# A streaming encoder step on one core: the mix stored in two parts, memory's products begun earlier, one score bank for two heads, four early output products

## The chip, the cores and the metric

The kernel runs on one core of one Trainium2 chip. The metric is the device time of one launch in microseconds; the time before is the median of three runs, 1799.81 us (1794.37 to 1802.57). One further execution was recorded by the hardware profiler, and every duration of an instruction comes from it.

## The reference

One layer of a hybrid encoder for two request groups that share the weights: a prompt of 1024 frames and a sample of 64 frames with caches, both of width 1024. All inputs and outputs are float32.

```python
h = rms_norm(x, g_norm1)
qa, ka, va, qb, kb, vb, logf = in_proj(h, w_in, ...)     # 8 + 8 heads of 64, QK-norm, forget logits
xp = xp + concat(band_attn(qa, ka, va, rel_bias), forget_attn(qb, kb, vb, logf)) @ w_o
mk, mv = mem_kv(mem_prompt, g_mem, w_mkv, g_mk)          # 256 memory tokens, 4 heads of 256
xp = xp + mem_attend(rms_norm(xp, g_norm2), mk, mv, w_mq, g_mq, w_mo)
xp = xp + conv_ffn(rms_norm(xp, g_norm3), prev, w_up, w_conv, b_conv, w_down)
# the sample rows: the same, but attention over cache + new rows (512 for heads A, 1024 for heads B),
# memory from its own cache, convolution from its own state
```

Outputs are both y, and the new keys, values, forget logits, memory keys and values and convolution states.

## The kernel before, in words

A float32 product is made of three TensorE products of "fp32r" parts: every operand is split into a high part (`act.copy` into an fp32r tile) and a low part (operand minus high part, by VectorE or GpSimd), and hi·hi, lo·hi and hi·lo are summed in one PSUM bank. Prompt and sample stand side by side as N = 1024 + 64 columns.

The program is one straight list of instructions. Its stages:

1. **Projection and prompt attention** (to about 565 us). Head pairs are projected one after the other, eight token tiles each (`proj`); the attention of finished pairs (`Attn`, 256 queries at a time) is woven between its matmuls by `weave`, which spreads a list of small steps (`subs`) over a list of main steps. `Attn.sum` ends each pair's block: the two heads' outputs are put into a 128x256 tile `mix`, which is stored to the DRAM tensor `mixd`.
2. **End of attention, memory's keys and values.** Memory (256 tokens) times `w_mkv` is a `line` of 64 pieces of six matmuls (8 column blocks n, 2 token tiles t, 4 pieces c). `load_wm` and `split_wm` fetch and split the weights, `mem_end` normalises a finished block and stores it, `mem_turn` transposes a key block for the DRAM copy `kmd`. `LEFT` says how many pieces stand beside each of the last substeps of attention.
3. **Sample attention**: eight `Sample` objects (head pairs, in the order `SAMPLES`). In step x of the loop the scores of sample x are made, the softmax, transposes and sums of sample x-1 are finished, and the caches of sample x+1 are loaded and split; `PER[x]` pieces of memory's line are woven between. `score(h)` runs once per head. It writes into rows of both heads, of which only the head's own 64 rows are read.
4. **Output projection** `project`: 24 `Product`s (8 blocks m of 128 rows, 3 chunks of 384, 384 and 320 columns, in `ORDER`), each 24 matmuls. The operand is the mix, in two parts `mixr`, with the samples' columns last (chunk 2). A finished product is added to the residual, stored to `x1d`, split into h2 and squared for the next norm. `Stream` fetches and splits the weights ahead.
5. Memory cross attention, feed-forward network and output, up to the end. The change leaves these as they are.

In between, `open_left` (once the line is used up) takes the place of memory's tiles, and loads the mix back in eight loads of 512 KB, four of them in flight, which ScalarE and VectorE split into `mixr`. The first product belongs to the last pass of the sample loop, the second follows it. `mixd`, `x1d`, `kmd` and `vmd` are DRAM tensors.

What sets the order: each engine runs its own list in program order and waits where an operand is not ready or a tile is not free. All data transfers here are issued by SyncE (SP) in one ordered list; an issue that waits holds back those behind it. A tile pool opened in the place of a closed one waits for what the closed one's tiles did. PSUM has eight banks of 2 KB per partition: two `pj`, two `PT`, one `tq`, one `O`, two `S`.

The lines that the text speaks of (numbers of the kernel before): L272 projection matmuls, L453/L508 prompt scores and sums, L520 the mix's store, L591 to L605 memory's inputs and weight splits, L615 memory's matmuls, L634 to L649 their ends, L709/L710 cache splits, L730 sample score matmuls, L733/L735 their reductions, L757 to L784 sample transposes, sums and outputs, L852 w_o's low part, L869 output matmuls, L908 to L912 the mix's loads and splits, L998 to L1015 the residual and what follows a product.

## Time and profile before

| | |
|---|---|
| median of three runs | 1799.81 us (1794.37 to 1802.57) |
| profiled execution, own time | 1798.58 us |
| its span, first to last instruction | 1796.5 us |
| mean granted TensorE clock | 0.991 |
| TensorE matmuls busy | 1718.8 us (96%) |
| VectorE busy | 1225.0 us (68%) |
| ScalarE busy | 930.5 us (52%) |
| GpSimd busy | 662.8 us (37%) |
| DMA | 200.12 MB, mean 111 GB/s |
| TensorE busy from 600 to 700 us | 88.81 of 100 |
| TensorE busy from 700 to 750 us | 43.17 of 50 |

How to read it: PE is TensorE's matmuls, PEld its weight loads, DVE VectorE, ACT ScalarE, POOL GpSimd, SP SyncE. Times are microseconds from the first instruction. "idle <-X" names what ended an engine's idle time. A group of instructions has its line, engine, operation, written tile <- read tiles and shapes, then its total and mean time (ns). The granted clock is the share of full speed that TensorE was given.

### The profile page before, as it was taken

The numbers are of one execution on the slowest core, as the hardware profiler recorded it, in microseconds if no ns is written. First come the engines' busy times: TensorE is split into PE (matmuls) and PEld (weight loads), VectorE is DVE, ScalarE is ACT, GpSimd is POOL, SyncE is SP. The second block draws the span as 40 slices with busy tenths as digits, with TensorE's granted clock in tenths as the row PEclk, the third lists the DMA queues.
The fourth block names the chain that finished last, engine by engine and source line by source line (L and its number), as shares of the span: only waits on it lengthen the run. The fifth ranks groups of instructions, "written<-read, shape, count | busy, mean of one in ns | idle before, by whom it ended". The sixth has DMA issues, their size and how long they took to land.

```text
span 1796.5 us, 34030 instructions
## 1 busy us (share of the span) xinstructions
PE 1718.8 (96%) x12412; PEld 1663.7 (93%) x12412; DVE 1225.0 (68%) x2710; ACT 930.5 (52%) x2042; POOL 662.8 (37%) x1025
## 2 busy tenths in 40 slices
PE   6899999999997888999999999999999999999999
PEld 5789999999997777999999999999999999999999
DVE  5877667677676797433444379877777777677994
ACT  5646666677676567433554456343333333433332
POOL 5746657878776554453443612100000000000000
PEclk9999999999999999999999999999999999999999
DMA  8312122122113777541111563222222222794232
GB/s 285 96 46 72 36 76 79 50 72 74 48 54 97 222 229 213 163 141 60 54 54 59 150 219 103 73 79 78 85 86 84 73 73 72 268 304 151 77 118 80
DMA packets 134103, 200.12 MB, mean 111 GB/s; under 512 B 20824, under 2 KB 73944, under 8 KB 133936
## 3 DMA queue, kind: packets, MB, share of 16 engines
q1 hardware_dynamic: 133936, 197.96, 34.9%
q8 instruction: 97, 1.59, 0.4%
q14 instruction: 70, 0.57, 0.1%
HBM read 155.61 MB, written 45.44 MB: 112 GB/s over the span
## 4 chain that ended last, share of the span: by engine, by line
PE 46%; DVE 3%; DMA 2%; issue 2%; POOL 1%; ACT 1%; SPq 0%; POOLq 0%; ACTq 0%; DVEq 0%
PE W L1381 25%; PE W L1678 9%; PE pj L869 7%; PE W L869 2%; DMA raw<-in_w_down_dram 1%; PE S L1124 1%; PE tq L1160 1%; PE O L1160 1%; POOL lo L852 1%; DVE lo L1246 0%; PE PT L1147 0%; DVE f L1246 0%; PE O L1124 0%; DMA kvraw<-in_w_down_dram 0%; DMA h<-ad 0%
## 5 line engine op out<-in xcount | busy, mean ns | idle before, releaser
L272 PE MATMUL pj<-whi,xhi 128*128 128x384 f32 (+1 forms) x512 | 194.9, 381 | 8.2 <-ACT xhi L130 7.1
L272 PE MATMUL pj<-wlo,xhi 128*128 128x384 f32 (+1 forms) x512 | 176.9, 346 | 3.2 <-POOL wlo L123 2.9
L272 PE MATMUL pj<-whi,xlo 128*128 128x384 f32 (+1 forms) x512 | 175.1, 342 | 4.2 <-DVE xlo L131 4.2
L1487 POOL COPY s<-gp 128x2 f32<-128x2 f32 x22 | 15.8, 718 | 335.0 <-DVE gp L1486 335.0
L458 ACT ACTIVATE s<-s,mx 128x640 f32<-128x640 f32 (+7 forms) x128 | 94.2, 736 | 80.1 <-DVE mx L456 78.4
L1381 PE MATMUL W<-h,hi 128*128 128x272 f32 x704 | 134.4, 288 | 1.4 <-ACT qlo L1517 1.4
L1678 PE MATMUL W<-f,hi 128*128 128x272 f32 x672 | 128.3, 288 | 3.2 <-DVE f L1246 3.1
L495 DVE TENSOR_TENSOR ptl<-PT,pth 128x512 fp32r<-128x512 f32 (+2 forms) x192 | 99.6, 522 | 37.8 <-ACT pth L494 35.4
L1381 PEld LDWEIGHTS W<-h,hi 128*128 128x128 f32 x704 | 110.8, 188 | 1.7 <-ACT qlo L1517 1.6
L1678 PEld LDWEIGHTS W<-f,hi 128*128 128x128 f32 x672 | 106.0, 189 | 3.8 <-DVE f L1246 3.3
L272 PEld LDWEIGHTS pj<-whi,xhi 128*128 128x128 f32 x512 | 99.5, 195 | 9.3 <-ACT xhi L130 7.1
L224 POOL TENSOR_TENSOR r<-m,mhalf 128x4 f32<-128x4 f32 (+1 forms) x72 | 73.8, 1025 | 91.4 <-DVE m L223 81.3
L272 PEld LDWEIGHTS pj<-wlo,xhi 128*128 128x128 f32 x512 | 99.2, 194 | 5.3 <-POOL wlo L123 4.4
L494 ACT CAST pth<-PT 128x512 fp32r<-128x512 f32 (+2 forms) x192 | 85.1, 449 | 36.9 <-PE PT L493 35.2
L272 PEld LDWEIGHTS pj<-whi,xlo 128*128 128x128 f32 x512 | 97.8, 191 | 5.1 <-DVE xlo L131 5.1
L1381 PE MATMUL W<-h,lo 128*128 128x272 f32 x352 | 101.8, 289 | 0.0
L1245 ACT CAST hi<-raw 128x512 fp32r<-128x512 f32 x68 | 42.2, 621 | 108.8 <-PE W L1381 58.2
L1678 PE MATMUL W<-f,lo 128*128 128x272 f32 x336 | 97.1, 289 | 0.0
L493 PE MATMUL PT<-ident,s 128*128 128x128 f32 x528 | 90.2, 276 | 5.0 <-DVE ptl L495 3.9
L227 POOL TENSOR_SCALAR qk<-qkraw,r 128x128 f32<-128x128 f32 x256 | 92.8, 379 | 6.0
L869 PE MATMUL pj<-a,hi 128*128 128x384 f32 (+1 forms) x352 | 89.5, 337 | 0.3 <-DVE qhi L1005 0.3
L453 PE MATMUL S<-kh,q 128*128 128x256 f32 (+1 forms) x304 | 76.9, 278 | 11.1 <-DVE mx L456 9.6
(604 smaller groups left out, 6053.0 us busy)
## 6 DMA issues: line engine op xcount, KB each, us to landing
raw<-in_w_down_dram SPq DMA_DIRECT2D x45, 256.0 KB, 3.1
wraw<-in_w_dram SPq DMA_DIRECT2D x56, 192.0 KB, 2.4
raw<-in_w_up_dram SPq DMA_DIRECT2D x41, 256.0 KB, 2.8
h<-ad SPq DMA_DIRECT2D x32, 272.0 KB, 4.7
mwraw<-in_w_mkv_dram SPq DMA_DIRECT2D x16, 512.0 KB, 5.1
raw<-in_w_mo_dram SPq DMA_DIRECT2D x32, 256.0 KB, 3.2
kvraw<-in_w_down_dram SPq DMA_DIRECT2D x32, 256.0 KB, 3.2
ad<-t SPq DMA_DIRECT2D x22, 272.0 KB, 2.1
```

Source lines behind the costliest of these rows:

```text
L224: pool.tensor_tensor(r[:rows], m[:rows], mhalf[:rows, 0:4], op=ALU.pow)
L227: pool.tensor_scalar(qk[:rows, h], raw[:rows, h * 64:(h + 1) * 64].rearrange("p (o d) -> p o d", o=1).broadcast_to([rows, 2, 64]), r[:rows ...
L272: pe.matmul(pj[:, :nw], x2[a][:, k, t * P:(t + 1) * P], wt[k][b][:, :nw], start=n == 0, stop=n == 3 * KT - 1)
L453: pe.matmul(sp[:, a:a + (k1 - k0) * P], q, kk[:, h, src], start=m == 0, stop=m == 1)
L458: act.activation(s[:, :n], s[:, :n], ACT.Exp, bias=mx, scale=-1.0, accum_out=sm)
L493: pe.transpose(pt[:, b - ch[0]], self.s[j][:, (b - w0) * P:(b - w0 + 1) * P], ident)
L494: act.copy(hi[:, f:f + n, j], pt[:, f:f + n])
L495: dve.tensor_tensor(lo[:, f:f + n, j], pt[:, f:f + n], f32(hi[:, f:f + n, j]), op=ALU.subtract)
L869: pe.matmul(out()[:, :cn], w[a][:, k % 4], x[b][k][:, c0:c0 + cn], start=k == 0 and n == 0, stop=k == KT - 1 and n == 2)
L1245: act.copy(hi, t)
L1381: pe.matmul(w[:, z, :Q], a(p, j), rights[j][b][:, z * Q:z * Q + Q], start=fresh and begin and j == 0 and x == 0, stop=final and end and j ...
L1678: pe.matmul(ws[m][:, z, :Q], la[p][:, m * P:(m + 1) * P], ra[b][:, z * Q:z * Q + Q], start=first and y == 0 and what in opening, stop=fina ...
```

## The change

1. **The mix in two parts.** `Attn.sum` splits each finished 128x256 mix at once (ScalarE copies the high part, GpSimd subtracts) and stores both. `mixd` has a first index for the part. `open_left` loads the columns of both parts straight into the product's operand tiles `ahi` and `alo`: six loads (two parts, chunks of 384, 384 and 256 columns) and no split. The samples' columns are split by one copy and one subtraction instead of eight each. `mix` has one buffer instead of two.
2. **Memory's inputs in their own places.** `memT` goes to two tiles of memory's pool (`mraw`, split in eight steps that are woven with the first substep) instead of borrowed `s` tiles; the weight tiles have four buffers instead of two, `kv` three instead of two. Several pools wait tile by tile (`reuse_waits="tile"`) for what lay in their place, not for a whole pool. The weight stream's pool is opened before memory's, so the first three w_o pieces are fetched earlier. `LEFT` and `PER` put 28 pieces beside the end of attention (15 before) and the rest into the first five sample steps. `mem_turn` comes two units late.
3. **Both heads' scores in one bank.** `score` runs once per sample. The query tile `zq` holds zeros in the places of the other head, so that one accumulation gives both heads' rows. One reduction over 128 rows stands where two over 64 were. Both caches are split ahead of it.
4. **Four early products.** (0,0), (0,1), (1,0) and (1,1), which need only prompt columns, run in the sample steps 6, 7 and 8 (`EARLY`), are added to the residual and stored to `x1d`. `project` loads these four back from `x1d`. All products use the two `pj` banks; before, the third and fourth used `PT`.

Three places of the new order follow, as the instructions stand in the program. On SP, from the loads of the eighth and last sample on, before the change (`mraw` is the mix, `raw` w_o's weights, `kraw` and `vraw` caches, `s` the bias rows):

```order
L670 DMA s<-rows 64x576 x2
L676 DMA kraw<-in_cak_dram 128x512 x2
L680 DMA vraw<-in_cav_dram 128x512
L638 DMA out_mv_dram<-kv 128x256
L639 DMA vmd<-kv 128x256
L908 DMA mraw<-mixd 128x1024
L638 DMA out_mv_dram<-kv 128x256
L639 DMA vmd<-kv 128x256
L899 DMA x_10572<-in_xT_dram 128x384
L843 DMA raw<-in_w_o_dram 128x512 x3
L908 DMA mraw<-mixd 128x1024 x4
```

And after it:

```order
L676 DMA s<-rows 64x576
L911 DMA ahi<-mixd 128x8x384
L911 DMA alo<-mixd 128x8x384
L911 DMA ahi<-mixd 128x8x384
L911 DMA alo<-mixd 128x8x384
L911 DMA ahi<-mixd 128x8x256
L911 DMA alo<-mixd 128x8x256
L676 DMA s<-rows 64x576
L682 DMA kraw<-in_cak_dram 128x512 x2
L686 DMA vraw<-in_cav_dram 128x512
L848 DMA raw<-in_w_o_dram 128x512 x3
```

The mix's loads have moved ahead of the caches of the seventh sample (the row of `kraw` here) and of the eighth.

On TensorE, behind the sums of the fifth sample (`O<-svh` is the last of them), after the change (`L874` is the output product's matmul, `L789` the transpose of the sample's output):

```order
L777 MATMUL O<-svh,pth 128x256
L777 MATMUL O<-svh,ptl 128x256
L874 MATMUL pj<-ahi,hi 128x384
L789 MATMUL PT<-ident,su 64x128
L874 MATMUL pj<-alo,hi 128x384
L874 MATMUL pj<-ahi,lo 128x384
```

The first two output products now stand here, ahead of the scores of the seventh sample; before, the first stood behind the last sums of the seventh sample.

On SP again, where the output projection begins, after the change (`L924` stores the early products, `L995` loads them back, `L997` is the residual, `L1001` the store of a product):

```order
L924 DMA x1d<-x_10862 128x384
L848 DMA raw<-in_w_o_dram 128x512
L995 DMA qhi<-x1d 128x384 x2
L848 DMA raw<-in_w_o_dram 128x512
L1054 DMA kvraw<-kmd 128x2x256
L848 DMA raw<-in_w_o_dram 128x512
L995 DMA qhi<-x1d 128x384
L1054 DMA kvraw<-vmd 128x2x256
L995 DMA qhi<-x1d 128x384
L848 DMA raw<-in_w_o_dram 128x512
L1054 DMA kvraw<-in_cmk_dram 128x2x256
L997 DMA qhi<-in_xT_dram 128x320
```

Four reloads stand ahead of the residual of the fifth product; before, the residual's loads began with the second product.

The diff, cut to its core:

```diff
-LEFT = (0, 0, 0, 15)
-PER = (4, 8, 9, 12, 6, 5, 6, 0, 0)
-STAGE, MIXES = 4, 8
+LEFT = (0, 7, 7, 7, 7)
+PER = (9, 9, 8, 7, 4, 0, 0, 0, 0)
+EARLY = {6: (0,), 7: (1,), 8: (2, 3)}
...
             if h == 1:
-                nc.sync.dma_start(mixd[p, :, g * 256:(g + 1) * 256], mix)
+                hi, lo = (wa.tile([P, 256], F32R, name=x) for x in ("mixh", "mixl"))
+                act.copy(hi, mix)
+                pool.tensor_tensor(lo, mix, f32(hi), op=ALU.subtract)
+                for z, part in enumerate((hi, lo)):
+                    nc.sync.dma_start(mixd[z, p, :, g * 256:(g + 1) * 256], f32(part))
...
+    wr = late_left.enter_context(tc.tile_pool(name="wr", bufs=1, side="left", reuse_waits="tile"))
...
+    mraw = [mp.tile([P, 4, 256], F32, name="mwraw", bufs=4) for _ in range(2)]
+    for z in range(2):
+        nc.sync.dma_start(mraw[z], i["memT"][4 * z:4 * z + 4].rearrange("k p t -> p k t"))
...
-        raw = mp.tile([P, 4, 256], F32, name="mwraw", bufs=2)
+        raw = mp.tile([P, 4, 256], F32, name="mwraw", bufs=4)
...
-                if c == 2 and u:
-                    mem_turn(*units[u - 1])
+                if c == 1 and u > 1:
+                    mem_turn(*units[u - 2])
...
-        def score(self, h):
+        def score(self):
...
+            for h in range(2):
+                q = self.z[:, 2 * h:2 * h + 2].rearrange("p h t -> p (h t)")
+                for m in range(2):
+                    first, last = h + m == 0, h + m == 2
+                    for c in range(self.nc):
+                        pe.matmul(sp[:, c], q, self.kc[h, c][m], start=first, stop=last)
+                    pe.matmul(sn[:, 0, :S], q, self.kn[m][:, h], start=first, stop=last)
...
-            dve.tensor_tensor_reduce(out=b[r, :n], in0=sf[r, :n], in1=b[r, :n], scale=-1.0, scalar=BIG,
-                                     op0=ALU.add, op1=ALU.min, accum_out=self.mx[r, 0:1])
+            dve.tensor_tensor_reduce(out=b[:, :n], in0=sf[:, :n], in1=b[:, :n], scale=-1.0, scalar=BIG,
+                                     op0=ALU.add, op1=ALU.min, accum_out=mx[:, 0:1])
...
+        ha = mixing.enter_context(tc.tile_pool(name="ha", bufs=1, side="left", reuse_waits="tile"))
+        tiles = [ha.tile([P, KT, N], F32R, name=x) for x in ("ahi", "alo")]
+        mixr.extend([t[:, k] for k in range(KT)] for t in tiles)
+        for c0, cn in CHUNKS:
+            for z, t in enumerate(tiles):
+                n = min(cn, T - c0)
+                nc.sync.dma_start(f32(t[:, :, c0:c0 + n]), mixd[z, :, :, c0:c0 + n].rearrange("k p t -> p k t"))
...
+    def early_product(n):
+
+        m, c = ORDER[n]
+        g = Product(2 * m, mixr, c, False)
+        cols = slice(c * 384, c * 384 + 384)
+        x = mq.tile([P, 384], F32, name="x1", bufs=2)
+        nc.sync.dma_start(x, i["xT"][m, :, cols])
+
+        def end():
+            dve.tensor_tensor(x, g.t[:, :384], x, op=ALU.add)
+            nc.sync.dma_start(x1d[m, :, cols], x)
+
+        return g.pieces[:-1] + [lambda: (g.pieces[-1](), end())]
...
-            if firsts and n == 0:
-                xr = early_x
+            if n < done:
+                nc.sync.dma_start(xo, out[m, :, c0:c0 + cn])
             else:
                 nc.sync.dma_start(xr, res[m, :, c0:c0 + cn])
-            if n < len(firsts):
-                g = firsts[n]
-            else:
-                g = Product(j + 2 * m, x, c, c == 2, "PT" if firsts and n < 4 else "pj")
-            yield g
...
+                g = Product(j + 2 * m, x, c, c == 2)
+                yield g
```

142 lines of the change are left out of this document (53 added, 89 removed).

## The prediction

> **What bounds the kernel now.** I read the page's head first, then the busy time by stretches, TensorE's waits, and the rows of the lines that the change touches.
>
> ```profile
> span 1796.5 us, 34030 instructions
> PE   6899999999997888999999999999999999999999
> DMA  8312122122113777541111563222222222794232
> 100.00:565.00 465.00, 455.56 (x3111) 433.71 (x3109) 327.18 (x932) 318.31 (x820) 334.95 (x610) 1.00 0.20 59
> 569.30:600.90 31.60, 18.10 (x117) 15.19 (x117) 19.72 (x41) 20.59 (x41) 16.99 (x21) 0.84 0.70 216
> 600.90:704.20 103.30, 91.20 (x640) 79.81 (x638) 83.89 (x203) 63.77 (x165) 49.87 (x49) 0.98 0.72 223
> 704.20:745.30 41.10, 35.21 (x191) 32.02 (x190) 24.85 (x51) 24.10 (x56) 17.61 (x13) 0.88 0.58 183
> ```
>
> The four stretches give, after their length, the busy time of PE, PEld, DVE, ACT and POOL, then the granted clock and the DMA share and rate. From 100 to 565 us (projection with prompt attention) PE is busy 455.56 of 465: it is the bound, and only about 9 us are open there. The dips of the PE line are the opening and slices 13 to 16, 560 to 745 us: the end of attention, the sample stage and the first output products. What the change can move in bulk is these 176 us. In them no engine is full, so one asks which wait ends last.
>
> ```profile
> PE O L508 <- ACT pth L494: 6.4, 2, 6.0
> PE S L453 <- DVE mx L456: 4.2, 3, 3.6
> PE PT L782 <- DVE su L778: 3.9, 2, 3.4
> 576.40 0.58 PE L508 MATMUL O<-pth,v 128*128 128x256 f32 x1 [6.04 <-ACT pth L494]
> 580.61 0.58 PE L453 MATMUL S<-kh,q 128*128 128x256 f32 x1 [3.63 <-DVE mx L456]
> 713.25 0.42 PE L782 MATMUL PT<-ident,su 128*64 128x128 f32 x1 [3.36 <-DVE su L778]
> 570.00:580.00 10.00, 0.94 (x5) 0.41 (x3) 3.90 (x9) 7.40 (x17) 6.61 (x10) 0.75 0.54 180
> 620.00:630.00 10.00, 7.43 (x49) 6.08 (x47) 9.16 (x24) 6.11 (x15) 4.75 (x4) 0.98 0.98 323
> 710.00:720.00 10.00, 5.36 (x17) 4.45 (x18) 8.24 (x10) 9.39 (x20) 6.28 (x4) 0.58 0.85 273
> ```
>
> The waits (total, times, longest) are many and short, with two large gaps: 570 to 580, where the attention of the last head has nothing beside it, and 710 to 720, where sample 7's end and the splitting of the mix share ACT and DVE and TensorE's clock falls to 0.58. Between them, at 620 to 630, DVE is 9.16 of 10 busy and the DMA at 0.98.
>
> On the clock, the page "TensorE: Matmul & The Clock Gate" of the Trainium skill (Part 1, "HAM oscillation — how this bites in real kernels") says that a gap of more than about 3.4 us halves it. This trace agrees: the 0.58 follows the 3.36 us wait.
>
> **The change, part by part.** The two stages that I cost are the time until memory's last product (t0; 704.1 now) and the time from there to the seventh output product, the first behind which PE runs without a gap (745.33 now). From there on, both kernels issue the same matmuls in the same order.
>
> ```profile
> L615 PE MATMUL pj<-mwhi,mlo x128: 278/282/382, 599.6 to 704.1; 128*128 128x256 f32 x128
> 737.14 0.51 PE L869 MATMUL pj<-a,hi 128*128 128x384 f32 x2
> 745.33 0.59 PE L869 MATMUL pj<-a,hi 128*128 128x384 f32 x2 [0.31 <-DVE qhi L1005]
> L733 DVE CUSTOM_DVE_ANT_0 s<-S,s 64x1024 f32<-64x1024 f32 x8 | 9.8, 1221 | 1.2 <-PE S L730 0.9
> L733 DVE CUSTOM_DVE_ANT_0 s<-S,s 64x512 f32<-64x512 f32 x8 | 5.5, 686 | 0.9 <-PE S L730 0.4
> L735 DVE CUSTOM_DVE_ANT_0 s<-tq,s 64x64 f32<-64x64 f32 x16 | 3.5, 218 | 0.1
> L710 DVE TENSOR_TENSOR kclo<-kraw,kchi 128x512 fp32r<-128x512 f32 x24 | 21.9, 930 | 2.0 <-ACT kchi L709 1.8
> L912 DVE TENSOR_TENSOR a<-mraw,a 128x1024 fp32r<-128x1024 f32 x8 | 11.1, 1394 | 1.8 <-ACT a L911 1.6
> L911 ACT CAST a<-mraw 128x1024 fp32r<-128x1024 f32 x8 | 8.3, 1044 | 0.4 <-DMA mraw<-mixd 0.2
> ```
>
> *Memory's line up to t0.* The table now puts 28 of the line's pieces beside the attention tail, up to 21 of them into the 570 to 600 us that are half empty, and the line ends in the fifth sample step instead of the seventh. So t0 comes before the scores of the sixth and seventh samples, not after. DVE is what I go by, since it is the fullest there. Its busy time from 569.3 to 704.2 is 19.72 + 83.89 = 103.6. Of this the shared bank takes away half of the score reductions of the first five samples: 4 long ones, 9.8/2 = 4.9, one short, 0.7, and 1.1 of the L735 ones, together 6.7 (a reduction over 128 partitions instead of 64 I take at the same time, as the rows of L456 with 128x1024 at 1220 ns beside 1221 here suggest). The sixth and seventh samples go behind t0: 4 cache splits of 0.93 (3.7), their scores (2.7) and about 3 of softmax and sums. That leaves 87.5. DVE idled 134.9 - 103.6 = 31.3 in that stretch. If it never idled, t0 would be 569.3 + 87.5 = 657; if all of the idling stayed, 688. I take half, since the cause of the two worst waits (ACT held by memory's inputs at 570) only moves with the inputs, which still can be loaded only once the last projection has read x: t0 = 672.5.
>
> ```profile
> L456 DVE CUSTOM_DVE_ANT_0 s<-S,s 128x1024 f32<-128x1024 f32 x2 | 2.4, 1220 | 1.1 <-POOL s L440 1.1
> 705.04 0.34 SPq L638 DMA_DIRECT2D out_mv_dram<-kv  x1
> L908 SPq DMA_DIRECT2D mraw<-mixd x5: 319/326/488, 699.3 to 715.6; - x5
> DMA to landing us min/median/max: 4.0/5.1/5.3
> kraw<-in_cak_dram SPq DMA_DIRECT2D x8, 256.0 KB, 3.3
> ```
>
> *The mix.* The eight ACT copies (8.3) and eight DVE subtractions (11.1) ahead of the first product vanish. In their place six loads fetch both parts, 2 x 8 x 128 x 1024 x 4 bytes = 8.4 MB where 4.2 MB were, of which 1.5 MB (three of the eight) had been fetched long before. They may be issued only when memory's tiles, whose place they take, are done with, and all of them stand in SP's queue ahead of the caches of the seventh sample. At the best rate of a 10 us window, 323 GB/s, that is 26 us; at 273 (the window where most of the mix is loaded now) 31. With 4 us until the first may start (the last store of memory's values must land, issued 705.04, a microsecond behind the last product, 2 to 3 us to landing) the first column chunk of both parts (3.1 MB) is there at t0 + 15, the second at + 25, the third at + 32, the seventh sample's cache (0.5 MB) at + 35. Two splits later it is scored, + 37; the eighth sample's cache lands 8 to 10 us behind (its 0.75 MB, and 0.75 to 1 MB of w_o's weights ahead of it), and the chain after that, reduction 0.7, exponential, scale, transposes, two sums, output transpose, takes 10 to 12. The four early products (4.2 us each, 16.8) fit into these waits and cost nothing of their own. So the fifth product, which needs every sample's columns, starts at t0 + 57 (50 to 61): 729.5. Before, it started at 737.1.
>
> ```profile
> L998 SPq DMA_DIRECT2D qhi<-in_xT_dram x11: 327/333/459, 729.6 to 767.7; - x11
> DMA to landing us min/median/max: 2.1/2.8/4.3
> L1008 ACT ACTIVATE hhi<-qhi,gcol x11: 563/616/618, 729.3 to 767.7; 128x384 fp32r<-128x384 f32 x8, 128x320 fp32r<-128x320 f32 x3
> L1009 DVE SCALAR_TENSOR_TENSOR hlo<-qhi,gcol,hhi x11: 553/619/1600, 730.0 to 768.4; 128x384 fp32r<-128x384 f32 x8, 128x320 fp32r<-128x320 f32 x3
> L1005 DVE TENSOR_TENSOR qhi<-pj,qhi x8: 492/558/558, 733.7 to 767.1; 128x384 f32<-128x384 f32 x6, 128x320 f32<-128x320 f32 x2
> ```
>
> *The early products' results* go to DRAM and come back. Four reloads stand on SP ahead of the residual's load for the fifth product, and they share two qhi buffers. The first pair is queued behind a weight load that waits for a buffer which the fifth product's own start frees, some 4 us after that start. Then come two rounds of load (2.8), cast (0.6), low part (0.6) and squares (0.5 on ACT for each of the pair, an estimate from the 0.6 of the cast), about 5 us each, then the fifth product's residual (2.8) and its addition (0.56): 4 + 5 + 5 + 2.8 + 0.6 = 17.4. The products now have two pj banks and no longer four with PT's, so the seventh waits for that addition: it starts about 17 us behind the fifth (12 if the reloads ran as one stream; 18.6 if each round takes 5.6), where 745.33 - 737.1 = 8.2 stood before. After such a gap I add 1.7, half of a 3.4 us stretch at half clock. So the seventh product starts at 672.5 + 57 + 17 + 1.7 = 748: + 3 against 745.3.
>
> ```profile
> L605 POOL TENSOR_TENSOR mwlo<-mwraw,mwhi 128x512 fp32r<-128x512 f32 x16 | 22.3, 1401 | 5.7 <-ACT rsq_y L77 2.9 <-ACT mwhi L604 2.3 <-DMA svn<-sv 0.4
> L231 POOL TENSOR_TENSOR ko<-qk,gk 128x128 f32<-128x128 f32 x1 | 0.5, 462 | 0.1
> L517 ACT COPY otmp<-O 64x256 f32<-64x256 f32 x5 | 1.8, 369 | 2.9 <-PE O L508 2.8
> PE pj L272 <- POOL wlo L123: 2.9, 4, 0.8
> L912 DVE TENSOR_TENSOR a<-mraw,a x8: 1203/1226/2128, 709.7 to 722.8; 128x1024 fp32r<-128x1024 f32 x8
> ```
>
> *The mix's split during attention* adds 32 times a copy on ACT (0.37, the 256-column row), a subtraction of 128x256 on POOL (between 0.46 and 1.40: 0.78) and one more store of 128 KB: 12 us of ACT, 25 of POOL, 4.2 MB over 540 us at a DMA share of 0.20. POOL is busy 334.95 of 465 there and ACT 318, so there is room, and PE's only wait for POOL's weight splits in that stretch is 2.9 us in sum. Hidden: 0. With the cover gone it would be up to 25 us; mix is single-buffered now, but a head's next use of it comes a whole attention block later.
>
> The page "SBUF — State Buffer" of the Trainium skill ("Who interferes with whom") speaks against this part: a DVE instruction with two SBUF inputs and a GpSimd instruction that reads SBUF shut each other out for a whole instruction. The trace bears a little of it: L912, which has two inputs in SBUF, has a shortest of 1203 ns and a longest of 2128. By the rule the 25 us on POOL would also be kept from DVE, which has 137.8 us free in the 465; the sum stays.
>
> Sum: + 3 on the profiled execution's 1798.6, and the same on the median of 1799.8: 1803.
>
> **Rivals.** *Faster: the line ends early and the rest follows.* With t0 at 657 and the reloads as one stream (12), the seventh product starts at 657 + 57 + 12 + 1.7 = 728, which is 17 less; with half of that, 9. For it: the 9.6 us of gaps at 570 to 580 have work put beside them, and DVE loses 20 us over the whole stage (11.1 of the mix, half of 9.8 + 5.5 + 3.5). Against: DMA. The stretch up to 704 moved 31.6 us x 216 GB/s + 103.3 us x 223 GB/s = 29.9 MB, and about 27 of it (without the early half of the mix and the last samples' caches) still precede t0, 84 us at 323 GB/s, so the feed must run near its best throughout. Time 1783 to 1791.
>
> *Slower: SP's queue.* One mechanism: 8.4 MB in one line, and caches and reloads stand behind it. If the transfers get the average rate of the old stage, 223 GB/s, the mix takes 38 us rather than 28, the last samples and the fifth product come 10 later and the seventh product at 758: 1812. It decides from about 250 GB/s downward. For it: 0.72 busy share at 223 with rows of 1.5 KB. Against: the 323 window.
>
> *Slower: POOL and ACT in the projection.* If a third of the 37 us of new work there lands on PE's path (a late wlo split, a late softmax scale), 12 us: 1815. It would show as PE waiting for POOL by over 9 us between 100 and 565. Against it stands the idle POOL quarter.
>
> *Nothing: the gain is hidden anyway.* The shared score bank, the dropped splits and the early line all save DVE and ACT time, but samples wait for DMA all along; then the stage ends within 4 us of the old one, which is close to my sum and is counted with it.
>
> **How the numbers follow.** A measurement of this kernel tells 0.5%, 9 us, from no change. No measurable change, with a sum of + 3: 0.42. Faster by the early line: 0.29. Slower: SP's queue 0.19, POOL and ACT 0.10. Likeliest time 1803; its own range, with t0 at 665 to 680, is 1795 to 1811. To hold eight in ten, the range reaches to the middle of the fast case and past both slow ones: 1781 to 1819.
>
> **What would show it.** Memory's last product between 665 and 680, the fifth output product 50 to 61 later, and a wait of PE's seventh product for DVE's addition of some 9 us. If memory's line ends before 660 or the reloads stream, the faster case holds. If the mix loads take over 35 us, or PE waits for POOL or ACT in the projection, a slower one does. DVE's score rows should show half the count at the same mean. A change after 760 us would not fit any of these.

## The result, and the profile after

The changed kernel takes 1826.98 us (median of 4 runs, 1824.09 to 1830.42) against 1799.08 for the kernel before (1794.37 to 1802.57): a ratio of 1.0158, interval 1.0127 to 1.0189. It is 28 us slower. The forecast was no measurable change, 1803, with 1781 to 1819 as the range; the measured time lies outside both.

The page of the changed kernel, span, TensorE and granted clock in 40 slices:

```profile
span 1828.6 us, 34101 instructions
PE   6899999999997997699999999999999999999999
PEclk9999999999999998799999999999999999999999
```

Counted from 1, as in the prediction, slice 13 is at 7 as before, slices 14 and 15 have risen from 8 to 9, and a deeper gap than before stands at slices 16 and 17 (686 to 777 us), with the clock down to 0.7 in the second of them. Behind it the two kernels run alike. The busy times by stretches of the changed kernel (length, then PE, PEld, DVE, ACT, POOL, the granted clock, DMA share and rate), cut at the last projection matmul (574.3), memory's last product (696.2), the fifth (755.2, cut at 755.6) and the seventh output product (773.7):

```profile
574.30:696.20 121.90, 103.91 (x724) 94.56 (x724) 92.50 (x193) 80.37 (x193) 66.30 (x72) 0.92 0.69 219
696.20:755.60 59.40, 46.19 (x201) 37.39 (x199) 18.43 (x55) 17.91 (x51) 9.50 (x11) 0.74 0.72 238
755.60:773.70 18.10, 7.17 (x48) 6.94 (x48) 4.67 (x8) 7.42 (x15) 9.88 (x8) 0.79 0.58 183
```

and the same stretch up to memory's last product in the kernel before, which begins at 566.1:

```profile
566.10:704.20 138.10, 112.51 (x781) 98.20 (x779) 106.20 (x252) 87.13 (x213) 67.76 (x70) 0.95 0.72 221
```

Memory's line does end earlier: 121.9 us behind the last projection matmul where it took 138.1. TensorE sat idle 18.0 us of that stretch (121.90 - 103.91), and 25.6 before (138.10 - 112.51). But this is paid back: from memory's last product to the seventh output product it is now 77.5 us, and it was 41.2 (745.33 - 704.1). The waits of TensorE between 100 and 900 us in the changed kernel, total, times and longest:

```profile
PE pj L874 <- DVE qhi L1000: 10.9, 1, 10.9
PE PT L493 <- DVE ptl L495: 10.8, 7, 4.3
PE S L453 <- DVE mx L456: 5.6, 7, 1.9
PE pj L621 <- DVE kv L640: 4.7, 3, 1.6
PE S L739 <- ACT kchi L716: 4.6, 2, 3.8
```

The first is the seventh product's wait for the fifth's addition, the second belongs to attention (half of it to its tail); it was 3.9 in the kernel before. Between memory's last product and the fifth output product VectorE, ScalarE and GpSimd are busy less than a third of the time (VectorE 18.43 of 59.40), TensorE 46.19 at a mean clock of 0.74, and the DMA stands at 0.72.

Where the 32.1 us between the two profiled executions came from (1828.6 - 1796.5): 8.2 up to the last projection matmul (574.3 against 566.1), 22.9 from there to the ninth output product (784.9 - 574.3 = 210.6 against 753.8 - 566.1 = 187.7), and 1.0 behind it.

### The profile page after: what moved, and what is told of

Its sections match the earlier page's. It is cut to its first block, busy times and chain, and to the rows that moved or that the text cites. A ratio compares the mean times of both kernels' runs of the same rounds, so it can differ in the third digit from the quotient of the medians.

```text
span 1828.6 us, 34101 instructions
## 1 busy us (share of the span) xinstructions
PE 1733.2 (95%) x12412; PEld 1677.1 (92%) x12412; DVE 1207.3 (66%) x2663; ACT 934.2 (51%) x2059; POOL 681.5 (37%) x1059
## 4 chain that ended last, share of the span: by engine, by line
PE 43%; DVE 6%; issue 2%; DMA 2%; POOL 1%; ACT 0%; SPq 0%; POOLq 0%; DVEq 0%; ACTq 0%
PE W L1373 24%; PE pj L874 7%; PE W L1670 7%; PE W L874 2%; DVE lo L1238 1%; PE S L1116 1%; PE tq L1152 1%; PE O L1152 1%; DVE f L1238 1%; DMA raw<-in_w_down_dram 1%; POOL lo L857 1%; DMA h<-ad 1%; PE PT L1139 0%; DVE f L1444 0%; PE O L1116 0%
## 5 line engine op out<-in xcount | busy, mean ns | idle before, releaser
L1237 ACT CAST hi<-raw 128x512 fp32r<-128x512 f32 x68 | 42.2, 621 | 109.3 <-PE W L1373 60.5
L227 POOL TENSOR_SCALAR qk<-qkraw,r 128x128 f32<-128x128 f32 x256 | 92.5, 379 | 6.0
L493 PEld LDWEIGHTS PT<-ident,s 128*128 128x128 f32 x528 | 67.4, 142 | 22.6 <-DVE ptl L495 16.8
```

Of the source, the lines that this page charges most:

```text
L227: pool.tensor_scalar(qk[:rows, h], raw[:rows, h * 64:(h + 1) * 64].rearrange("p (o d) -> p o d", o=1).broadcast_to([rows, 2, 64]), r[:rows ...
L493: pe.transpose(pt[:, b - ch[0]], self.s[j][:, (b - w0) * P:(b - w0 + 1) * P], ident)
L1237: act.copy(hi, t)
```

## The experiments

All times are medians beside runs of the kernel before on the same chip. The first 116 us differ by up to 3.5 us between profiled executions of kernels that are alike there (the changed kernel is 1.6 behind the kernel before at 116, e17 3.5), so stages are measured from the last projection matmul to the ninth output product ("the stage"), read off TensorE's timeline:

| run | us | ratio to before (interval) | the stage, us |
|---|---|---|---|
| before | 1798 to 1801 | 1 | 187.7 |
| changed | 1826.98 | 1.0158 (1.0127 to 1.0189) | 210.6 |
| e1 store only | 1809.76 | 1.0056 (1.0036 to 1.0076) | 192.1 |
| e2 later store | 1828.49 | 1.0159 (1.0130 to 1.0187) | 206.7 |
| e3 raw mix | 1816.26 | 1.0089 (1.0061 to 1.0117) | 203.0 |
| e4 caches first | 1827.44 | 1.0154 (1.0129 to 1.0179) | 209.5 |
| e5 pinned store | 1841.77 | 1.0226 (1.0208 to 1.0244) | 216.1 |
| e6 four banks | 1828.00 | 1.0145 (1.0124 to 1.0166) | 205.9 |
| e7 no early | 1827.45 | 1.0148 (1.0131 to 1.0164) | 207.3 |
| e8 score only | 1800.79 | 0.9997 (0.9985 to 1.0009) | 187.7 |
| e9 work only | 1804.13 | 1.0019 (1.0009 to 1.0028) | 190.0 |
| e10 old table | 1833.83 | 1.0180 (1.0159 to 1.0202) | 211.7 |
| e11 combination, old table | 1808.90 | 1.0042 (1.0027 to 1.0058) | 195.5 |
| e12 combination, new table | 1811.16 | 1.0050 (1.0030 to 1.0069) | 197.0 |
| e13 memory's places | 1808.40 | 1.0046 (1.0028 to 1.0064) | 194.2 |
| e14 direct load | 1804.85 | 1.0028 (1.0015 to 1.0041) | 192.7 |
| e15 staged, old table | 1807.87 | 1.0042 (1.0027 to 1.0057) | 195.7 |
| e16 staged, new table | 1813.55 | 1.0079 (1.0064 to 1.0094) | 198.3 |
| e17 e13, two subtractions moved | 1801.05 | 1.0007 (0.9996 to 1.0019) | 188.0 |
| e18 changed, the same moved | 1828.64 | 1.0150 (1.0120 to 1.0180) | 208.0 |

The stage is read from a single execution of each kernel. How far such a reading can be trusted shows in e2: its instructions stand in the same order as those of the changed kernel on every engine, apart from 20 of SyncE's 933 places, and its time is the same, but its stage is 3.9 us shorter. A difference of up to 4 us in the last column therefore tells nothing by itself.

### The loss in the projection: e1, e9, e2, e5

What stands in the trace of the changed kernel near 180 us, SyncE's list first (start, length), then VectorE:

```profile
174.91 0.33 SPq L524 DMA_DIRECT2D mixd<-mixh  x1
177.03 0.32 SPq L524 DMA_DIRECT2D mixd<-mixl  x1
177.40 0.92 SPq L114 DMA_DIRECT2D wraw<-in_w_dram  x2
178.42 0.38 SPq L405 DMA_DIRECT2D bias<-rows  x1
```

```profile
183.06 0.11 DVE L406 MEMSET bias<- 64x64 f32 x1 [4.21 <-DMA bias<-rows]
```

and in the kernel before:

```profile
172.34 0.33 SPq L520 DMA_DIRECT2D mixd<-mix  x1
172.76 1.35 SPq L114 DMA_DIRECT2D wraw<-in_w_dram  x3
174.93 0.33 SPq L405 DMA_DIRECT2D bias<-rows  x1
```

```profile
178.13 0.11 DVE L406 MEMSET bias<- 64x64 f32 x1 [1.33 <-DMA bias<-rows]
```

The low part's store waits for GpSimd's subtraction, and in SyncE's list two weight loads and the bias load of the next head pair stand behind it. VectorE fills the corners of that bias tile, and everything of VectorE stands behind the fill. The fill waits 2.9 us longer than before; of this 1.4 is the load itself, which lands 4.5 us behind its issue where it took 3.1. e1 adds only the split and its store to the kernel before (and, as in the changed kernel, `mix` has one buffer):

```diff
+                hi, lo = (wa.tile([P, 256], F32R, name=x) for x in ("mixh", "mixl"))
+                act.copy(hi, mix)
+                pool.tensor_tensor(lo, mix, f32(hi), op=ALU.subtract)
                 nc.sync.dma_start(mixd[p, :, g * 256:(g + 1) * 256], mix)
+                nc.sync.dma_start(mixld[p, :, g * 256:(g + 1) * 256], f32(lo))
```

> The kernel before, with only the split of each finished mix added (ScalarE's copy, GpSimd's subtraction, one more store, the low part's, on SyncE's queue; mix single-buffered); nothing reads the low part back. Theory (the low part's store waits for GpSimd in SyncE's list and holds back the bias load behind it, for which VectorE waits): about 8 us slower than before, all of it before 570 us, with VectorE waiting for a bias load for 3 to 4 us near 180 and 250. Rival (the added work is hidden, and the 8 us come from the other changes' order): within 2 us of before.

It is 10 us slower than before; 5.2 of this arise between 116 and 536 us (6.6 in the changed kernel). The theory had all of it before 570 us, but in its profiled execution the stage behind that is 4.4 us longer as well, about as much as two executions can differ by. e9 takes the one store out again and leaves the copy and the subtraction:

```diff
-                nc.sync.dma_start(mixld[p, :, g * 256:(g + 1) * 256], f32(lo))
```

> The kernel before, with ScalarE's copy and GpSimd's subtraction of each finished mix, but without the low part's store (the parts are read by nothing); the whole mix is stored as before. Theory (SyncE's list waits for GpSimd at the low part's store): within 2 us of before, the last projection matmul at 567 to 568. Rival (the added work itself is on the path): as with the store, 574 to 575, and 1809.

3.4 us slower than before, where the theory allowed 2, and 1.2 of it between 116 and 536. VectorE's idle time that a bias load ended, between 100 and 300 us (total, times), in before, the changed kernel, e1 and e9, in this order:

```profile
  DMA bias<-rows: 5.8, 4
```

```profile
  DMA bias<-rows: 10.5, 4
```

```profile
  DMA bias<-rows: 10.1, 4
```

```profile
  DMA bias<-rows: 5.7, 4
```

So the store, not the work, is what delays the bias loads, and two thirds of e1's loss go with it; the last third stays with the copy, the subtraction and the single buffer. The 4.7 us that these waits grew by in the changed kernel are most of its 6.6. TensorE meets them as a wait for `ptl`, which VectorE makes: 5.8 of the 5.9 us after the change fall at 176 to 190 and 246 to 260 us, where before there were none. Between 100 and 565 us, before and after:

```profile
PE PT L493 <- DVE ptl L495: 1.9, 5, 0.4
```

```profile
PE PT L493 <- DVE ptl L495: 5.9, 5, 2.7
```

The two runs that meant to move the store are of less use. e2 issued both stores half an attention block later:

```diff
+                while stores:
+                    stores.pop()()
...
-                    nc.sync.dma_start(mixd[z, p, :, g * 256:(g + 1) * 256], f32(part))
+                stores.append(lambda p=p, g=g, parts=(hi, lo): [...])
```

> The changed kernel, with both stores of a finished mix issued half an attention block later, when the data has long been there; the same copies, subtractions and transfers. Theory (SyncE's list waits for GpSimd): the last projection matmul comes 6 to 8 us earlier than in the changed kernel, 1819 to 1821. Rival (GpSimd's and ScalarE's added work itself is on the path): no change, 1827.

No change, but it tells nothing: the scheduler that orders the instructions had moved the stores back, and SyncE's list had them ahead of the same bias loads as before. e5 pinned them in the order in which they are written:

```diff
-    ... [nc.sync.dma_start(mixd[z, p, :, g * 256:(g + 1) * 256], f32(part)) ...
+    ... [tc.keep_in_program_order(nc.sync.dma_start(mixd[z, p, :, g * 256:(g + 1) * 256], f32(part))) ...
```

> The changed kernel, with both stores of a finished mix issued half an attention block later and pinned there in SyncE's list (in the run of the later stores, the scheduler had put them back where they were, ahead of the bias loads). Now both bias loads of a head pair stand ahead of the next stores. Theory (the low part's store waits for GpSimd and holds the bias load behind it back): VectorE's waits for a bias load near 180 and 250 us fall to those of the kernel before, the last projection matmul comes at 567 instead of 574, 1819 to 1821. Rival (GpSimd's and ScalarE's work itself): no change, 574 and 1827.

Now 12 to 15 us slower than the changed kernel, where the theory had it 6 to 8 faster. Both bias loads did move ahead of the stores, and VectorE's waits for them fell from 10.5 to 7.6, but the second load is held in SyncE's list, and with it all that stands behind:

```profile
173.62 8.77 SPq L405 DMA_DIRECT2D bias<-rows  x2
```

What holds it there (the last reader of its tile, by the order of the program) was not tested. The run refutes the simple repair and leaves the cause to e1 and e9.

### The mix's loads: e3, e4

e3 undoes the split: the mix is stored and loaded whole, into the low part's tile, and split in place.

```diff
+            raw = tiles[1][:, :, c0:c0 + n]
+            nc.sync.dma_start(f32(raw), mixd[:, :, c0:c0 + n].rearrange("k p t -> p k t"))
...
+    def split_mix(hi, lo):
+        act.copy(hi, f32(lo))
+        dve.tensor_tensor(lo, f32(lo), f32(hi), op=ALU.subtract)
```

> The changed kernel, with the mix stored and loaded once, unsplit (4.2 MB in three loads into the low part's tile), and split there in place by 12 copies on ScalarE and 12 subtractions on VectorE while both are idle. Theory (the 8.4 MB ahead of the last samples' caches, and the split's store, cost time): 8 us back in the projection, and 12 us between memory's last product and the fifth output product, together about 1807. Rival (the time behind memory's last product goes into the chain of samples and reloads, not the transfers): 8 us back only, 1819.

10.7 us faster than the changed kernel: the projection's loss is gone, and memory's last product to the fifth output product takes 7.8 us less (51.2 against 59.0, and 59.1 in e2, so this part repeats well). Theory and rival had 12 and 0 for it. In the changed kernel the two second-chunk loads and those of the third hold SyncE back 2.3 to 4.3 us each, and the low part's three land 10.7 to 16.3 us after their issue. SyncE's list and the rows of that tile:

```profile
703.47 4.33 SPq L911 DMA_DIRECT2D alo<-mixd  x1
707.85 4.11 SPq L911 DMA_DIRECT2D ahi<-mixd  x1
720.00 1.01 SPq L682 DMA_DIRECT2D kraw<-in_cak_dram  x2
```

```profile
DMA to landing us min/median/max: 10.7/14.1/16.3
```

The seventh sample's cache is issued at 720.0, 20 us behind the mix's first load (699.97). e4 issues it ahead of them:

```diff
-        if not line and ha is None:
-            ha = open_left()
...
             nxt.load()
+        if not line and ha is None:
+            ha = open_left()
```

> The changed kernel, with the seventh sample's loads issued ahead of the mix's loads instead of behind them. Theory (samples wait in the one queue behind 8.4 MB): the seventh sample is scored about 20 us earlier, beside the mix's landing, but the eighth still waits behind the mix; 5 us less, 1822. Rival (the eighth sample decides alone): no change. If the first early products come later by the 0.7 MB ahead of them and that decides, 2 us more.

No change in the time: the rival. The seventh sample was scored at 709.1 instead of 727.9, as the theory had it, but the eighth sample's cache was still issued behind the mix, at 735.1 (734.7 in the changed kernel), and that sample was scored at 739.6 (740.7).

### The early products: e6, e7

e6 puts the fifth and sixth output product in the PT banks:

```diff
-                g = Product(j + 2 * m, x, c, c == 2)
+                g = Product(j + 2 * m, x, c, c == 2, "PT" if done and n < done + 2 else "pj")
```

> The changed kernel, with the fifth and sixth output product in the two PT banks, which nothing else uses then, so that the seventh waits for no addition. Theory (the 10.9 us wait is the reload chain through two pj banks): the seventh product starts some 7 us behind the fifth instead of 18; the chain itself stays, so the ninth waits for what is left of it, 3 us or less: 8 us less, 1819. Rival (what waits behind is only moved to the ninth product): 3 us less.

The seventh product now starts 7.3 us behind the fifth, as the theory had it, but the wait moved to the ninth product and lost only 2 us (10.86 in the changed kernel, 9.88 in e3):

```profile
782.56 0.63 PE L874 MATMUL pj<-ahi,hi 128*128 128x320 f32 x1 [8.71 <-DVE qhi L1000]
```

The run's time does not change; the rival had 3 us. So the chain of reloads and additions itself is late, and more banks only shift who meets it. e7 leaves the early products out:

```diff
-EARLY = {6: (0,), 7: (1,), 8: (2, 3)}
+EARLY = {}
...
-    for g in project(0, mixr, ORDER, 4, ...
+    for g in project(0, mixr, ORDER, 0, ...
```

> The changed kernel without the early products: all 24 in the projection, no reload. Theory (the early products fill waits, the reloads give most of it back): 16.8 us of matmuls move behind the last sample, the reload wait of 10.9 us and its half clock go: 3 to 5 us slower than the changed kernel, 1831. Rival (early products pay in full): 17 slower, 1844. Other rival (they cost more than they give, since products and samples get into each other's way): 1822 or less.

No change in the time, where theory and rival had 3 to 5 and 17 us more. Two products run early even so (712.4 and 720.3), moved up ahead of the last samples by the scheduler. So four early products with their reloads are worth no more than two without.

### The score bank and the table: e8, e10

e8 is the kernel before with `score` of the changed kernel (shown in the diff above) and both cache splits ahead of it.

> The kernel before, with only the shared score bank (and both caches of a sample split ahead of its score). Theory (VectorE is not what the sample stage waits for): within 4 us of before, 1796 to 1803, although VectorE's busy time falls by 9 us. Rival (VectorE's reductions are on the path there): 6 to 9 us faster, 1791.

No change: ratio 0.9997. The reductions have half the count at the same mean, as priced (VectorE, 560 to 735 us of e8):

```profile
L736 DVE CUSTOM_DVE_ANT_0 s<-S,s 128x1024 f32<-128x1024 f32 x4 | 4.9, 1225 | 1.7 <-PE S L733 1.1 <-PE tq L734 0.6
L736 DVE CUSTOM_DVE_ANT_0 s<-S,s 128x512 f32<-128x512 f32 x4 | 2.8, 689 | 1.7 <-PE S L733 1.6
```

The 9 us that VectorE saves on the reductions are not what the stage waits for. e10 is the changed kernel with the table of the kernel before:

```diff
-LEFT = (0, 7, 7, 7, 7)
-PER = (9, 9, 8, 7, 4, 0, 0, 0, 0)
-EARLY = {6: (0,), 7: (1,), 8: (2, 3)}
+LEFT = (0, 0, 0, 15, 0)
+PER = (4, 8, 9, 12, 6, 5, 5, 0, 0)
+EARLY = {7: (0, 1), 8: (2, 3)}
```

> The changed kernel with the table of the kernel before for memory's pieces (none beside the first four substeps of the attention tail, 15 beside the last, the rest up to the seventh sample step), the mix's loads and the early products therefore behind the eighth sample's loads. Theory (the early line only moves the samples behind it, where they form a chain with nothing beside it, and so the new table is what lost most): 10 to 15 us less than the changed kernel, 1812 to 1817. Rival (the table gains the 16 us by which memory's line ends earlier): 10 us slower, 1837.

Neither: 1.0180 against 1.0158, intervals overlapping, the stage 1 us longer. With the old table the line ends 142.9 us behind the last projection matmul, with the new one 121.9. Ending it 21 us earlier gains nothing, and neither does it lose: what the line's time loses comes back behind it.

### What was left: e11 to e18

e11 and e12 combine e3, e7 and two more banks for the third and fourth product, with the old and the new table.

```diff
-EARLY = {6: (0,), 7: (1,), 8: (2, 3)}
+EARLY = {}
...
-                g = Product(j + 2 * m, x, c, c == 2)
+                g = Product(j + 2 * m, x, c, c == 2, "PT" if order is ORDER and n in (2, 3) else "pj")
```

> The changed kernel with the mix stored whole and split in place, no early products, the third and fourth output product in the PT banks, and the old table: of the change, memory's inputs in their own places, the pools' waits by tile, the shared score bank and the direct load are left. If memory's places and the direct load are worth anything by themselves: 1790 to 1797. If not: 1800.

> The same with the new table of memory's pieces. Theory (the table loses): 5 to 12 us slower than with the old table. Rival (the table gains once split and reloads are gone): 5 or more us faster than with the old table.

8 to 11 us slower than before remain, more than either expectation for e11 had, and the tables differ by 2, within what these runs can tell, where theory and rival for e12 had 5 and more either way. What is left of the change in e11 is memory's own places, the waits by tile, the load into memory's place, and the score bank, which e8 shows to be worth nothing. e13 gives the kernel before only memory's places (own tiles, four weight buffers, three kv, splits beside the first substep, transposes two units late, waits by tile in memory's pool):

```diff
+    mraw = [mp.tile([P, 4, 256], F32, name="mwraw", bufs=4) for _ in range(2)]
...
-        raw = mp.tile([P, 4, 256], F32, name="mwraw", bufs=2)
+        raw = mp.tile([P, 4, 256], F32, name="mwraw", bufs=4)
...
-                if c == 2 and u:
-                    mem_turn(*units[u - 1])
+                if c == 1 and u > 1:
+                    mem_turn(*units[u - 2])
...
+    splits = [lambda k=k: split_mem(k) for k in range(KT)] + [lambda: split_wm(0, 0), lambda: split_wm(0, 1), lambda: load_wm(1, 0), lambda: load_wm(1, 1)]
+    weave(substeps(), splits)
```

> The kernel before, with only memory's inputs in their own places: own tiles for memory, split beside the first substep, four weight buffers, three kv, the transposes two units late, tile-wise waits in memory's pool; the old table. Theory (what is left of the loss behind the attention, 8 us from the last projection matmul to the ninth output product, comes from the mix's loads waiting for memory's tiles): no change, 1797 to 1803, the ninth product 187 us behind the last projection matmul. Rival (memory's splits hold up the attention tail and memory's line): 4 to 6 us slower, 1805.

8 us slower: the rival, which had 4 to 6. e14 gives it only the load into memory's place, whole and split in place:

```diff
-            raws[k] = stage.tile([P, T], F32, name="mraw", bufs=STAGE)
+            raws[k] = f32(mixr[1][k][:, 0:T])
```

> The kernel before, with the whole mix loaded straight into the low part's tiles and split there in place, so that no load can begin before memory's last product (in the kernel before, three of eight lie in staging tiles 120 us earlier). Theory (as above): 5 to 8 us slower, 1805 to 1808, the first product 16 to 18 us behind memory's last instead of 10. Rival: no change.

4 to 5 us slower; the first product came 13.5 behind memory's last and not 16 to 18, and the loss shows later, as a wait of 4.9 for an addition at the seventh product. Why the addition is late there stays open. e15 and e16 add to e11 and e12 an early load of the first column chunk into a tile of its own:

```diff
+    stage = mq.tile([P, KT, 384], F32, name="stage")
...
+            if c0 == 0:
+                mixsplits.extend(lambda k=k: split_from(tiles[0][:, k:k + 2, :384], tiles[1][:, k:k + 2, :384], stage[:, k:k + 2]) for k in range(0, KT, 2))
+                continue
...
+        if x == 4:
+            nc.sync.dma_start(stage, mixd[:, :, 0:384].rearrange("k p t -> p k t"))
```

> The kernel of the combination with the old table, with the first column chunk of the mix loaded whole into a staging tile while samples still run, and (1,0) as second product, so that the first two products need nothing that waits for memory's tiles but their own operand places. Theory (the late loads): the first product 5 to 8 us behind memory's last, 1800 to 1803. Rival (memory's line ends too late anyway): 1807.

> The same with the new table, and the seventh sample's loads ahead of the mix's. Theory (with the first chunk there and half the bytes behind it, the chain of samples seven and eight decides): 1801 to 1806. Rival (the early line pays at last): 1795 or less.

Neither gained; e15's first product stood 14.8 us behind memory's last, not 5 to 8, and e16's 14.9. That chunk was not what held it; what did stays open. e16 is 6 us slower than e15; it has the new table and the seventh sample's loads moved, and which of the two costs this was not tested.

What e13 loses shows at two instructions. VectorE and GpSimd of e13 around 582 us:

```profile
581.32 6.78 DVE L238 SCALAR_TENSOR_TENSOR mlo<-mwraw,gcol,mhi 128x256 fp32r<-128x256 f32 x2
588.02 0.28 DVE L495 TENSOR_TENSOR ptl<-PT,pth 128x128 fp32r<-128x128 f32 x1
```

```profile
581.05 0.45 POOL L231 TENSOR_TENSOR ko<-qk,gk 64x128 f32<-64x128 f32 x1
...
585.09 1.25 POOL L605 TENSOR_TENSOR mwlo<-mwraw,mwhi 128x512 fp32r<-128x512 f32 x1
586.30 0.28 POOL L440 TENSOR_SCALAR_AFFINE_SELECT s<-s 128x128 f32<-128x128 f32 x1
586.56 1.25 POOL L605 TENSOR_TENSOR mwlo<-mwraw,mwhi 128x512 fp32r<-128x512 f32 x1
```

Two low parts of memory take 6.78 us, the first 2.55 and the second 4.31 (the rows of this tile: shortest, median, longest; and the second by itself):

```profile
L238 DVE SCALAR_TENSOR_TENSOR mlo<-mwraw,gcol,mhi x8: 471/483/4309, 574.1 to 583.8; 128x256 fp32r<-128x256 f32 x8
583.79 4.31 DVE L238 SCALAR_TENSOR_TENSOR mlo<-mwraw,gcol,mhi 128x256 fp32r<-128x256 f32 x1
```

The second ends (588.1) just after GpSimd's row of instructions ends (587.8). The same 2.55 and 4.3 stand in the changed kernel (from 586.96 on, the second ending at 593.74, GpSimd's row at 593.45), and TensorE's 4.29 us wait for `ptl` at 593.99 follows them. In the kernel before, the eight take 476 to 487 ns. e17 and e18 take two instructions out of that row:

```diff
-        (dve if y % 2 else pool).tensor_tensor(lo, raw, f32(hi), op=ALU.subtract)
+        (dve if y % 2 or n == 0 else pool).tensor_tensor(lo, raw, f32(hi), op=ALU.subtract)
```

> The kernel of memory's own places alone, with the low parts of the first memory weights made by VectorE instead of GpSimd (two subtractions of 1.25 us leave GpSimd's row of back-to-back work at 579 to 588 us). Theory (VectorE's last low part of memory, with two inputs in SBUF, is shut out for as long as GpSimd's row of instructions lasts, and took 4.31 us instead of 0.48): that instruction ends 2.5 us earlier, its longest falls to about 1.8 us, TensorE's wait for ptl there from 4.5 to about 2, and the run is 3 us faster, 1805. Rival (it waits for something else, such as its data or a store): 4.3 us as before and no change, 1808.

> The changed kernel with the same edit. Theory: the longest low part of memory falls from 4.3 to about 2 us (w_o's first low part may take the free place on GpSimd: then 3), TensorE's longest wait for ptl from 4.3 to 2, and 2 to 4 us are saved, 1824. Rival: no change.

In e17 GpSimd's row ends at 585.42, and the second instruction at 585.27:

```profile
585.07 0.35 POOL L440 TENSOR_SCALAR_AFFINE_SELECT s<-s 128x128 f32<-128x128 f32 x1
```

```profile
581.20 4.08 DVE L238 SCALAR_TENSOR_TENSOR mlo<-mwraw,gcol,mhi 128x256 fp32r<-128x256 f32 x2
583.67 1.60 DVE L238 SCALAR_TENSOR_TENSOR mlo<-mwraw,gcol,mhi 128x256 fp32r<-128x256 f32 x1
```

```profile
L238 DVE SCALAR_TENSOR_TENSOR mlo<-mwraw,gcol,mhi x8: 470/480/2554, 574.4 to 583.7; 128x256 fp32r<-128x256 f32 x8
```

The longest of the group, 2.55, is now the first of the two, which the edit left as it was. The second fell from 4.31 to 1.60: 2.7 us, where the two subtractions taken out of the row make 2.5. e17 takes 1801.05, ratio 1.0007 (0.9996 to 1.0019): e13's loss of 7 to 8 us is gone. The rival (waiting for data) would have kept 4.3. The edit also takes work off GpSimd, but TensorE does not wait less for GpSimd's weight splits: 0.5 us between 610 and 712 in e13, 2.1 in e17. How 2.7 us at one instruction become 7 is only in part seen: TensorE's longest wait for `ptl` there falls from 4.5 to 1.8, the clock granted from 590 to 600 us rises from 0.72 to 0.98 (from 580 to 590 it stays at 0.5), and memory's line ends 135.1 us behind the last projection matmul instead of 142.3.

In e18 the second low part fell in the same way (4.32 to 1.60), and TensorE's longest wait for `ptl` in the tail from 4.3 to 1.6. But memory's last product came no earlier, 122.1 us behind the last projection matmul against 121.9 (120.2 in e2), and the run's time did not change. So the held instruction is what e13 loses by, but in the changed kernel no gain from releasing it is seen, though one of a few us could hide in these intervals. No version beat the kernel before; e17 and e8 are level with it.

## Why the prediction was wrong

**"Hidden: 0" for the split during attention** is the first step that failed. The prices were right (GpSimd's subtraction took 0.74, 0.78 was taken), and the idle time was there. The step counted busy time and left out the queue: the new store waits for GpSimd in SyncE's list, and the bias loads stand behind it. The changed kernel lost 6.6 us between 116 and 536, and was 8.2 late at the last projection matmul, with 1.6 of that from the opening; e1 lost about 10, of which 7 go with the store (e9). The prediction followed SyncE's queue for the reloads, and did not do it for the store. The rival for this stage had the right sign (12 us, chance 0.10) but the wrong place: TensorE's wait for GpSimd's weight splits stayed at 2.8 us; what grew was its wait for `ptl`, from 1.9 to 5.9, behind VectorE, behind a bias load.

**"DVE is what I go by, since it is the fullest there", with half of its idle time**, for memory's last product at 672.5, is the second and the larger: 15.5 us of the 23.7 that it came late. VectorE was not the fullest. By the prediction's own rows TensorE's matmuls were busy 18.10 + 91.20 = 109.3 us from 569.3 to 704.2, and VectorE 103.6. In the changed kernel TensorE is busy 103.91 us from the last projection matmul to memory's last product. 672.5 lies 106.4 us behind that matmul as it stood before, so it would have left TensorE 2.5 us idle where it had 25.6; the idle time came down to 18.0. (Busy time is as measured, at a mean clock of 0.92; how much of it a full clock would save was not measured.)

VectorE's work was sized well: 92.5 us between 574.3 and 696.2, where the forecast, counted from 566.1, has 87.5 + 2.6 = 90.1. But 5.9 of the 92.5 are the time by which two low parts were held, and its idle time hardly fell: 121.9 - 92.5 = 29.4, against 138.1 - 106.2 = 31.9. The upper end, 688, plus the 8.2 of the projection is 696, which is what came; this does not show that VectorE set it. The two gaps at 570 to 580 went, and a new one came in their place, made by the very splits that were put there (e13, e17): VectorE held for 4.31 us, TensorE 4.29, and the clock at 0.55 around and behind it:

```profile
590.00:600.00 10.00, 6.01 (x32) 6.01 (x33) 7.66 (x10) 4.15 (x8) 4.20 (x6) 0.55 0.56 192
```

Since e18 shortened this gap and the line did not end earlier, which waits set its end in the changed kernel stays open; those left between 610 and 712 are short, 3.8 us in total for the largest kind in e18.

The page "SBUF — State Buffer" of the Trainium skill ("Who interferes with whom"), which the prediction weighed against the mix's subtraction and set at nothing, names this exclusion. The runs agree that VectorE is shut out in such a pair, but at another pair of instructions than the one that was looked at, and for longer than the one instruction that the prediction took from the page.

**What followed was nearly right, in part by luck.** The first output product came 15.2 us behind memory's last (711.5; forecast 15), the fifth product 59.0 (57), the seventh 18.5 behind the fifth (17), with a wait of 10.86 where some 9 was named:

```profile
773.69 0.66 PE L874 MATMUL pj<-ahi,hi 128*128 128x384 f32 x1 [10.86 <-DVE qhi L1000]
```

(The forecast compares by count: before, the product that needs every sample's columns is the fourth, at 733.6.) Inside the 59.0 two errors cancel: the seventh sample was scored at 31.7 instead of 37, and from there to the fifth product it took 27.3 instead of 20. The 1.7 us for the clock was put ahead of the seventh product; the half clock came behind its start, and lasted longer. That product took 7.1 us at a mean clock of 0.57 where it took 4.3 before, which is 2.8.

So the waits and reloads behind memory's line, which the prediction set as losses, came about as priced, and the gain that they were set against, 704.1 to 672.5, came only to 696.2. At the seventh output product the forecast was 3 us behind the kernel before, and the run is 28.4 behind (773.7 against 745.3). The 25.4 between them are 23.7 at memory's last product (8.2 of it up to the last projection matmul), 2.0 more to the fifth product and 1.5 more to the seventh, less the 1.7 that the forecast had allowed there for the clock.

**The rivals.** The faster case needed memory's line to end before 660 and did not come. SyncE's queue as the forecast gave it (the loads at 223 GB/s instead of 323) did not happen: 710 to 730 moved at 371 and 353 GB/s, and the mix landed 26.1 us behind its first issue. The nothing-gained rival was right on the score bank (e8) and, unexpectedly, on the table (e10).

Parts of the change, each added alone to the kernel before: split and store 10 us (e1), memory's places 8 (e13), the direct load 4 to 5 (e14). They need not add up to the 28, as e18 shows for memory's places, and reloads and early products hardly show in a time by themselves (e6, e7). How the 28 us divide among the parts is not settled.

## What to carry to other kernels

A store or load added to an in-order queue is a wait for its producer, placed ahead of everything behind it: look up who is next in that list before calling spare engine time a cover. Before taking one engine as the bound of a stage, add up the busy time of all of them, and see what idle time the forecast would leave to each. Filling a gap with work is not the gap gone: take the idle time of the old stage as kept until a named wait is shown to end, and see which engine the filler shares. A wait that was the loss in one version need not be it in the next (e17, e18). Ending one stage early gained nothing here (e10), since the stage behind it gave the time back.

## What the runs showed of the hardware

A VectorE instruction with two operands in SBUF, the on-chip memory that the engines share (128x256, 0.48 us alone) took 4.31 us beside GpSimd instructions without a break, while four whole ones of GpSimd went by, and ended 0.29 us behind the last of them (e13; the same in the changed kernel). With two of the four taken out it took 1.60 (e17, e18). So it can be held for more than one instruction. Nor does it always wait for the end of the row: the one ahead of it took 2.55 and ended with GpSimd's row still going on for 4 us, and in e17 and e18 the second ended 0.15 us ahead of the row's end. In these cases it ended while GpSimd ran its `affine_select` (L440), which took 0.48 and 0.35 us there instead of 0.28; but another of these, at 586.30 in e13, went by. What lets it in is not shown.

The DMA reached more than the 323 GB/s that the kernel before shows, with rows of 1.5 KB while the mix was loaded:

```profile
710.00:720.00 10.00, 9.36 (x33) 8.22 (x33) 0.44 (x2) 0.82 (x4) 0.00 (x0) 0.58 1.07 371
```
